# One queue for ScalarE's copies in the attention, and a reordered start, in a one-core encoder layer

## The chip, the core and the metric

The kernel runs on one core of a Trainium2 chip. A core has TensorE (PE, matrix products), VectorE (DVE), ScalarE (ACT), GpSimd (POOL) and SyncE (SP, which here only issues transfers), each with its own instruction stream, and 16 DMA engines. The metric is the device time of one execution in microseconds, lower is better.

## The reference

One layer of a streaming encoder on 2048 rows of width 1024, all in float32. In short:

```
mod = silu(c) @ w_ada + b_ada            # 6 x 1024: shift, scale, gate, twice
h = rmsnorm(x, g_norm1) * (1 + sc1) + sh1
q_sb, k_sb, v_sb, q_ca, k_ca, v_ca = split(h @ w_in)          # 8 heads of 64 each
o_sb = stick_breaking_attention(q_sb, k_sb, v_sb)             # strictly causal
o_ca = chunked_relpos_attention(rms(q_ca), rms(k_ca), v_ca, rel_bias)   # own chunk of 64 + 8 before it
x = x + gt1 * (concat(o_sb, o_ca) @ w_o)
h = rmsnorm(x, g_norm2) * (1 + sc2) + sh2
x = x + gt2 * (square(relu(h @ w1)) @ w2)
```

## The kernel before, in words

The rows are worked in four blocks of 512 (`TB`), in reversed order, transposed: 128 partitions hold 128 of the 1024 columns, so x of a block is eight tiles (`KT = 8`) of 128x512. Every float32 product of importance is made as three products of float32r parts: a copy to float32r ("hi", on ACT), the difference ("lo", on DVE or POOL, helper `split`), and `mm3`, which is hi by hi, hi by lo, lo by hi.

**Start.** TensorE first runs products of a tile of ones into a scrap bank (`keep_busy`, tile `idle`). Meanwhile SP loads the eight x tiles of block 3, with c between the sixth and the seventh, broadcast to 128 partitions (tile `cb`, 512 KB). ACT squares the x tiles, DVE adds the squares (`nsaa`), TensorE sums them over partitions (`norm_columns`, `pva`), DVE and POOL make the reciprocal root, ACT spreads it on a diagonal (`ndga`), and a product with ones gives it in all partitions (`norm_spread`, `pra`). ACT makes sigmoid(c), DVE multiplies by c into `cs`. The modulation columns are made as they are needed: `ada_column(j)` multiplies the 128x1024 tile `wa<j>` of the transposed w_ada by `cs` and sums along the row, one custom DVE instruction each (in the trace `wa<-wa,cs,bcol`). Then comes a loop over the eight k tiles: each needs its w_in columns (`wf`, split into `wfirst` and `wide`), two modulation columns (KT+k for the scale, k for the shift) and its normalized x (`ht`), and feeds 18 products into six banks (`pq`).

**Projections.** The other blocks and column groups follow, some postponed into the attention.

**Attention.** 112 units (stick-breaking `SB(h, g, c)`: head, query block, key block; chunked `CA(h, g)`) of four steps each, 448 steps, query blocks 2 and 3 first, then 1, then 0. At each step, in a written order: TensorE transposes the weights of the unit eight steps back (`wt`), the softmax work of this step runs (ACT `z`, DVE scan `p`, POOL `b` for SB; DVE, ACT `e`, POOL for CA), ACT and DVE split the transposed weights (`wth`, `wtl`), jobs left over from earlier steps run (list `soon`), TensorE multiplies weights with values (`acc`, two banks in turn) and makes the next scores, and `fill` puts as many products of postponed projections (`pf`, banks) and output projections (`po`, rows) as the plan's shares allow. A few jobs wait a counted number of steps in `later`.

When the last product of a head and query block is in, `finish` copies the two halves of its bank out, in two following steps (`otmp`, then `o`, ACT, 64x512 each), POOL adds them, and after every second head `keep` splits the pair (`os`) and stores it. Only after both copies can the bank be used again. Of a postponed projection's bank, ACT copies the hi part (`st` or `svf`) and a later job makes the lo part and stores it. A bank copy that meets a `finish` in one step waits a step; other meetings are let be. The output projections of blocks 2 and 3 also square their new rows and make the second norm's reciprocal root (`second`, `powers`, `spread`, `third`: tiles `pvm`, `nym`, `ndgm`, `prm`). The wrapper `Ordered` keeps an engine's instructions in the written order; SP's transfers in the attention go around it.

**After the attention.** The rest of block 1's output projection (`po`) runs as loads for block 0's output projection (`opm` from `scr_m`, weights `ow`) come in; then the MLP, by far the longest stage, with products of summed operands in the manner of Strassen.

Of the kernel before, what the change touches and what calls it, by code (L numbers as in the profile page):

```python
# [18 lines left out]
P = 128  # L19
# [60 lines left out]
def encoder_kernel(ctx, tc, xs, c, g1, g2, w_in, w_first, w_rest, gqk, bias, w_o, w1, w2, w_ada, b_ada, out):  # L80
# [163 lines left out]
    if True:  # L244
# [5 lines left out]
        padn.tile([P, 32], F32, tag="pad", name="padn")  # L250
# [5 lines left out]
        cb = stp.tile([P, D], F32, tag="bg", name="cb", bufs=2)  # L256
        cg = stp.tile([P, D], F32, tag="bg", name="cg", bufs=2)
# [247 lines left out]
        keep_busy(36, idle)  # L505
        act.activation(cg[:, 0:1], zero, AF.Sigmoid)
        for j in range(3):
            load_x_pair(3, j, osp)
        osp.dma_start(cb, c.partition_broadcast(P))
# [6 lines left out]
        def load_first(k):  # L516
            if k % 2 == 0:
                wraw.append(ring.tile([P, 2, 3, CW], F32, tag="r8", name=f"wf{k}"))
            if k:
                osp.dma_start(wraw[-1][:, k % 2], w_first[:, k])  # L520
            for j in (KT + k, k):
                adas[j] = adaw.tile([P, D], F32, tag="wa", name=f"wa{j}")
                osp.dma_start(adas[j], w_ada[j * P : (j + 1) * P, :])
            if not k:
                osp.dma_start(wraw[-1][:, k % 2], w_first[:, k])
# [16 lines left out]
        def silu(i):  # L542
            dve.tensor_tensor(*(t[:, i * TB : (i + 1) * TB] for t in (cs, cg, cb)), op=ALU.mult)
# [47 lines left out]
        first_w(1)  # L591
        for k in range(KT):
# [6 lines left out]
            for j in (KT + k + 1, k + 1) if k + 1 < KT else ():  # L599
# [7 lines left out]
            if k == 0:  # L607
                dve.tensor_copy(r3, p3)
# [12 lines left out]
            for m, p in enumerate(first):  # L621
                hi, lo = [w2s[k // 2][:, k % 2, l] if p == 2 else wide[:, k, l, p] for l in range(2)]
                for n in range(2):
                    cl = slice(n * P, (n + 1) * P)
                    mm3(
                        pss[2 * m + n], hi[:, cl], lo[:, cl], hts[3][k][:, 0, :], hts[3][k][:, 1, :],
                        k == 0, k == KT - 1,
                    )
# [80 lines left out]
    if True:  # L709
# [36 lines left out]
        def finish(u):  # L746
# [23 lines left out]
        def keep(u, o):  # L770
# [3 lines left out]
            q = act if u is units[-1] else sp  # L774
# [6 lines left out]
        class Unit:  # L781
# [26 lines left out]
            def values(self, j):  # L808
# [351 lines left out]
        def finish_row(g, n, ps, xr):  # L1160
# [93 lines left out]
        late, soon, first = [], [], []  # L1254
# [30 lines left out]
        def load(u):  # L1285
            need = (10,) if u.ca else (2, 3, 0, 1) + ((4,) if u.g == 0 else ())
            if u.g < 2:
                while not all((p, u.g) in have for p in need):
                    for job in soon:
                        job()  # L1290
                    soon.clear()
# [34 lines left out]
        for i in range(len(steps) + LAG):  # L1326
# [40 lines left out]
        while soon:  # L1367
            soon.pop(0)()
# [742 lines left out]
def _lay_out(i):  # L2111
# [6 lines left out]
        "c": i["c"][0],  # L2118
# [32 lines left out]
```

## Time and profile before

| | us |
|---|---|
| median of 3 runs (2524.98 to 2527.75) | 2527.54 |
| the profiled execution | 2525.42 |
| its span, first to last instruction | 2523.7 |
| PE busy, of the span | 2503.5 (99%) |
| DVE busy | 2034.2 (81%) |
| ACT busy | 1523.1 (60%) |
| POOL busy | 773.8 (31%) |

Times in the profile count from the span's start. A row of a timeline gives the start, the length, the engine, the operation with what it writes and reads, the form, how many, and in brackets the idle time of the engine before it with what ended it. A row of the waits names who waited for whom, the total, the number of times and the longest. A row of a table by stretches gives each engine's busy time and instruction count, then the granted TensorE clock, the busy share of the DMA engines and what they moved in GB/s. Most rows carry line 42, the wrapper's, so tiles tell instructions apart. A busy PE is not proof of useful work: at the start it is busy with the `idle` products.

### The profile page before, as it was taken

The numbers are of one execution on the slowest core, as the hardware profiler recorded it, in microseconds if no ns is written. First come the engines' busy times: TensorE is split into PE (matmuls) and PEld (weight loads), VectorE is DVE, ScalarE is ACT, GpSimd is POOL, SyncE is SP. The second block draws the span as 40 slices with busy tenths as digits, with TensorE's granted clock in tenths as the row PEclk, the third lists the DMA queues.
The fourth block names the chain that finished last, engine by engine and source line by source line (L and its number), as shares of the span: only waits on it lengthen the run. The fifth ranks groups of instructions, "written<-read, shape, count | busy, mean of one in ns | idle before, by whom it ended". The sixth has DMA issues, their size and how long they took to land.

```text
span 2523.7 us, 39531 instructions
## 1 busy us (share of the span) xinstructions
PE 2503.5 (99%) x12384; PEld 2093.8 (83%) x12384; DVE 2034.2 (81%) x3580; ACT 1523.1 (60%) x2917; POOL 773.8 (31%) x1156
## 2 busy tenths in 40 slices
PE   9999999999999999999999999999999999999999
PEld 7888888888888888888888888888888888888787
DVE  7656776887789888999858777779877859799998
ACT  6333424778876687666855555567555546576665
POOL 4330154776776677776620000000000000010000
PEclk9999999999999999999999999999999999999999
DMA  9879968789888788866787878996998996887882
GB/s 369 322 297 362 356 270 292 233 256 315 260 260 252 246 250 252 278 194 206 219 304 254 301 285 316 331 352 189 326 328 270 315 365 260 315 252 278 310 275 83
DMA packets 296547, 706.29 MB, mean 280 GB/s; under 512 B 32016, under 2 KB 88336, under 8 KB 284688
## 3 DMA queue, kind: packets, MB, share of 16 engines
q1 hardware_dynamic: 290432, 690.64, 79.5%
q0 software_dynamic: 4608, 8.39, 1.9%
q10 hardware_dynamic: 1296, 4.72, 0.5%
q8 instruction: 98, 1.61, 0.3%
q14 instruction: 113, 0.93, 0.1%
HBM read 476.61 MB, written 227.02 MB: 279 GB/s over the span
## 4 chain that ended last, share of the span: by engine, by line
PE 87%; DVE 7%; DMA 2%; ACT 1%; issue 1%; SPq 0%; POOL 0%; DVEq 0%; ACTq 0%; POOLq 0%
PE ps L42 25%; PE ps_s L42 15%; PE pt L42 11%; PE acc L42 7%; PE wt L42 7%; PE pf L42 5%; PE z L42 5%; PE po L42 4%; PE pq L42 3%; DVE opr L42 2%; PE pso L42 2%; PE cz L42 2%; DVE ol L42 1%; PE ct L42 1%; DVE r L42 1%
## 5 line engine op out<-in xcount | busy, mean ns | idle before, releaser
L42 ACT CAST wth<-wt 128x512 fp32r<-128x512 f32 (+3 forms) x544 | 257.7, 484 | 177.6 <-PE wt L42 164.7
L42 PE MATMUL ps<-h,opw 128*128 128x512 f32 x1512 | 358.6, 389 | 0.0
L42 DVE TENSOR_TENSOR wtl<-wt,wth 128x512 fp32r<-128x512 f32 (+3 forms) x544 | 291.7, 548 | 66.9 <-ACT wth L42 63.2
L42 POOL TENSOR_TENSOR b<-p 128x512 f32<-128x512 f32 (+1 forms) x320 | 292.0, 912 | 155.8 <-DVE p L42 103.5
L42 PEld LDWEIGHTS ps<-h,opw 128*128 128x128 f32 x1512 | 283.7, 188 | 58.8
L42 PE MATMUL pt<-w,ht 128*128 128x512 f32 x1248 | 288.2, 391 | 0.0
L42 PE MATMUL ps_s<-h,opw 128*128 128x512 f32 x1152 | 277.1, 389 | 0.0
L42 PEld LDWEIGHTS pt<-w,ht 128*128 128x128 f32 x1248 | 233.0, 188 | 47.7
L42 DVE TENSOR_TENSOR_SCAN p<-z,p,zero 128x512 f32<-128x512 f32 x192 | 245.5, 1280 | 20.1 <-ACT z L42 17.4
L42 PEld LDWEIGHTS ps_s<-h,opw 128*128 128x128 f32 x1152 | 216.0, 188 | 45.0 <-DVE cp L42 0.2
L42 ACT CAST opr<-r 128x512 fp32r<-128x512 f32 x280 | 174.3, 623 | 129.1 <-PE ps L42 71.4
L42 PE MATMUL ps<-opr,ol 128*128 128x512 f32 x960 | 222.0, 390 | 0.4 <-DVE opr L42 0.3
L42 PE MATMUL acc<-wth,v 128*128 128x512 f32 (+3 forms) x544 | 221.3, 410 | 0.2
L42 PEld LDWEIGHTS ps<-opr,ol 128*128 128x128 f32 x960 | 179.8, 188 | 40.2 <-DVE opr L42 1.9
L42 ACT ACTIVATE z<-z 128x512 f32<-128x512 f32 (+1 forms) x320 | 166.6, 521 | 54.1 <-PE z L42 49.5
L42 DVE TENSOR_TENSOR opr<-r,opr 128x512 fp32r<-128x512 f32 x280 | 188.5, 704 | 10.7 <-ACT opr L42 9.9
L42 PE MATMUL acc<-wtl,v 128*128 128x512 f32 (+3 forms) x544 | 185.5, 347 | 0.1
L42 PE MATMUL z<-k,q 128*128 128x512 f32 (+3 forms) x640 | 183.1, 368 | 1.5 <-DVE p L42 1.5
L42 POOL DMA_DIRECT2D scr_x<-txu x12 | 10.5, 879 | 546.6 <-ACT txu L42 529.2
L42 PE MATMUL ps<-oph,opv 128*128 128x512 f32 x768 | 175.5, 390 | 0.5 <-DVE txo L42 0.2
L42 PE MATMUL wt<-ident,b 128*128 128x128 f32 x1088 | 170.8, 272 | 1.5 <-DVE p L42 1.5
L42 PEld LDWEIGHTS wt<-ident,b 128*128 128x128 f32 x1088 | 137.2, 140 | 39.9 <-DVE p L42 2.2
(226 smaller groups left out, 5063.9 us busy)
## 6 DMA issues: line engine op xcount, KB each, us to landing
r<-scr_hid SPq DMA_DIRECT2D x80, 512.0 KB, 6.6
q<-scr_q SPq DMA_DIRECT2D x128, 256.0 KB, 5.2
w<-in_w_dram SPq DMA_DIRECT2D x64, 512.0 KB, 5.8
k<-scr_k SPq DMA_DIRECT2D x240, 128.0 KB, 4.3
v<-scr_v SPq DMA_DIRECT2D x120, 256.0 KB, 4.3
wa<-in_w_ada_dram SPq DMA_DIRECT2D x48, 512.0 KB, 6.3
ow<-scr_wo SPq DMA_DIRECT2D x24, 1024.0 KB, 6.5
l<-scr_t SPq DMA_DIRECT2D x20, 1024.0 KB, 7.4
```

What stands on the lines that cost most here:

```text
L42: return lambda *x, **y: self.tc.keep_in_program_order(f(*x, **y))
```

## The change

In the start, c is loaded as 128x8 columns (32 B to a partition) from ACT's queue instead of a broadcast of 512 KB on SP's; its silu is made on 8 columns, spread on eight diagonals by DVE and POOL, and eight products with ones give `cs`. There are 14 idle products in place of 36, and 9 more behind the new ones. The second tile's w_in part is loaded after its w_ada tiles, the first columns are made in another order, half the diagonal of the norm is made on POOL, the copy `r3` moves from DVE to ACT, and in the first two k tiles all products with the hi part of `ht` come before those with the lo part.

In the attention, `finish`, its second copy, `keep` and the bank copies go into one list, `heavy`, of which one runs per step, two when more than three wait, and none in the last two steps of a diagonal SB unit unless more than three wait. Block 0's chunked heads store through POOL's queue, except the last. The second norm of block 3 starts 14 steps after its last square instead of 3, and both norms' diagonals are made in two halves, a step apart, with the product one step later.

```diff
-        cb = stp.tile([P, D], F32, tag="bg", name="cb", bufs=2)
-        cg = stp.tile([P, D], F32, tag="bg", name="cg", bufs=2)
+        cg = stp.tile([P, KT, P], F32, tag="bg", name="cg", bufs=2)
...
-        keep_busy(36, idle)
-        act.activation(cg[:, 0:1], zero, AF.Sigmoid)
+        keep_busy(14, idle)
+        act.dma_start(ccol[:, 0], c)
+        act.activation(cg[:, 0, 0:1], zero, AF.Sigmoid)
         for j in range(3):
             load_x_pair(3, j, osp)
-        osp.dma_start(cb, c.partition_broadcast(P))
...
-            if k:
+            if k > 1:
                 osp.dma_start(wraw[-1][:, k % 2], w_first[:, k])
...
-            if not k:
+            if k < 2:
                 osp.dma_start(wraw[-1][:, k % 2], w_first[:, k])
...
+        act.activation(ccol[:, 1], ccol[:, 0], AF.Sigmoid)
+        dve.tensor_tensor(ccol[:, 1], ccol[:, 1], ccol[:, 0], op=ALU.mult)
+        for i, e in ((0, dve), (KT // 2, pool)):
+            ks = slice(i, i + KT // 2)
+            e.tensor_tensor(
+                cg[:, ks], ident.unsqueeze(1).to_broadcast([P, KT // 2, P]),
+                ccol[:, 1, ks].unsqueeze(2).to_broadcast([P, KT // 2, P]), op=ALU.mult,
+            )
+        for k in range(KT):
+            pe.matmul(cs[:, k * P : (k + 1) * P], ones, cg[:, k], start=True, stop=True)
+        keep_busy(9, idle)
...
-        more_squares(1, 6)
-        act.activation(cg, cb, AF.Sigmoid)
-        silu(0)
-        more_squares(6, KT)
-        silu(1)
+        more_squares(1, KT)
...
+        ada_column(KT, adas[KT])
         dve.tensor_scalar(v3, pv[:, 0:4], 1.0 / D, EPS, op0=ALU.mult, op1=ALU.add)
         pool.tensor_tensor(y3, v3, mhalf[:, :4], op=ALU.pow)
-        ada_column(KT, adas[KT])
+        ada_column(0, adas[0])
...
-        for i in range(4):
+        for i in range(2):
             act.activation(dg[:, i, :], ident, AF.Copy, scale=y3[:, i : i + 1])
-        ada_column(0, adas[0])
+            pool.tensor_tensor(dg[:, i + 2, :], ident, y3[:, i + 2 : i + 3].to_broadcast([P, P]), op=ALU.mult)
         first_scale(0)
+        ada_column(KT + 1, adas[KT + 1])
...
+        act.copy(r3, p3)
...
-            for j in (KT + k + 1, k + 1) if k + 1 < KT else ():
+            for j in ((KT + k + 1, k + 1) if k else (1,)) if k + 1 < KT else ():
...
-                dve.tensor_copy(r3, p3)
...
+                    if k > 1:
+                        mm3(ps, hi[:, cl], lo[:, cl], hts[3][k][:, 0, :], hts[3][k][:, 1, :], False, k == KT - 1)
+                        continue
+                    pe.matmul(ps, hi[:, cl], hts[3][k][:, 0, :], start=k == 0, stop=False)
+                    pe.matmul(ps, lo[:, cl], hts[3][k][:, 0, :], start=False, stop=False)
+            for m, p in enumerate(first) if k < 2 else ():
+                hi = w2s[k // 2][:, k % 2, 0] if p == 2 else wide[:, k, 0, p]
+                for n in range(2):
+                    pe.matmul(pss[2 * m + n], hi[:, n * P : (n + 1) * P], hts[3][k][:, 1, :], start=False, stop=False)
...
-                    wait({3: 6, 0: 2}.get(u.g, 4), lambda: keep(u, o))
-
-            soon.append(rest)
+                    wait({3: 6, 0: 2}.get(u.g, 4) - 1, lambda: heavy.append(lambda: keep(u, o)))
+
+            heavy.append(rest)
...
-            q = act if u is units[-1] else sp
+            q = act if u is units[-1] else pool if u.ca and u.g == 0 else sp
...
-                    done = lambda: finish(self)
-                    done.ends = True
-                    soon.append(done)
+                    soon.append(lambda: heavy.append(lambda: finish(self)))
...
-                    later.add(3, second)
+                    later.add(14 if g == 3 else 3, second)
...
-                dg = norm_diagonal(op, y, f"m{g}", op.tile([P, TB], F32, tag="otmp", name=f"ndgm{g}"))
-                later.add(2, lambda: third(dg))
+                dg = op.tile([P, TB], F32, tag="otmp", name=f"ndgm{g}").rearrange("p (a b) -> p a b", b=P)
+
+                def part(i):
+                    dve.tensor_tensor(
+                        dg[:, i : i + 2], ident.unsqueeze(1).to_broadcast([P, 2, P]),
+                        y[:, i : i + 2].unsqueeze(2).to_broadcast([P, 2, P]), op=ALU.mult,
+                    )
+
+                part(0)
+                later.add(1, lambda: part(2))
+                later.add(3, lambda: third(dg))
...
-            ends = any(hasattr(job, "ends") for job in done)
             for job in done:
-                if ends and hasattr(job, "bank"):
-                    soon.append(job)
+                if hasattr(job, "bank"):
+                    heavy.append(job)
                 else:
                     job()
+            short = front is not None and not front.ca and front.diag and fs > 1
+            for _ in range(max(0, len(heavy) - 3) if short else min(len(heavy), 1 + (len(heavy) > 3))):
+                heavy.pop(0)()
...
-        "c": i["c"][0],
+        "c": col(i["c"][0]),
```

More of the change, by code (lines that the diff above doesn't have):

```diff
@@ L249, in encoder_kernel @@
         padn = pa.enter_context(tc.tile_pool(name="padn", bufs=1))
-        padn.tile([P, 32], F32, tag="pad", name="padn")
+        ccol = padn.tile([P, 32], F32, tag="pad", name="padn")[:, : 2 * KT].rearrange("p (a k) -> p a k", k=KT)
         stp = pa.enter_context(tc.tile_pool(name="stp", bufs=6))
@@ L540, in more_squares @@
                 dve.tensor_tensor(acc, acc, sq, op=ALU.add)
-        def silu(i):
-            dve.tensor_tensor(*(t[:, i * TB : (i + 1) * TB] for t in (cs, cg, cb)), op=ALU.mult)
-        more_squares(1, 6)
-        act.activation(cg, cb, AF.Sigmoid)
-        silu(0)
-        more_squares(6, KT)
-        silu(1)
+        more_squares(1, KT)
         pv = norm_columns(pq, acc, "a3")
@@ L623, in encoder_kernel @@
                 for n in range(2):
[L624 to L628, printed above, removed]
+                    cl, ps = slice(n * P, (n + 1) * P), pss[2 * m + n]
+                    if k > 1:
[7 more added lines that the diff above has]
+                    pe.matmul(pss[2 * m + n], hi[:, n * P : (n + 1) * P], hts[3][k][:, 1, :], start=False, stop=False)
         free[0] += 4
@@ L1253, in encoder_kernel @@
         rest = 0
-        late, soon, first = [], [], []
+        late, soon, first, heavy = [], [], [], []
         def fill(part, more=0):
@@ L1288, in load @@
                 while not all((p, u.g) in have for p in need):
-                    for job in soon:
-                        job()
-                    soon.clear()
+                    while soon or heavy:
+                        (heavy or soon).pop(0)()
                     force(filler[0])
@@ L1366, in encoder_kernel @@
             value(u, j)
-        while soon:
-            soon.pop(0)()
+        while soon or heavy:
+            (heavy or soon).pop(0)()
         later.flush()
```

## The prediction

> **What bounds the kernel now.** I read the page first, then the stretches, then TensorE's waits, then the timeline where the change acts.
>
> ```profile
> span 2523.7 us, 39531 instructions
> PE 2503.5 (99%) x12384; PEld 2093.8 (83%) x12384; DVE 2034.2 (81%) x3580; ACT 1523.1 (60%) x2917; POOL 773.8 (31%) x1156
> ...
> L42 POOL DMA_DIRECT2D scr_x<-txu x12 | 10.5, 879 | 546.6 <-ACT txu L42 529.2
> ```
>
> TensorE is busy nearly throughout, so nothing that shortens another engine's work shortens the kernel by itself. The sum below was made against the execution with this span, which took 2525.42 us; the median of the runs is 2527.54, 2.1 us above it, and I carry the difference over to the median unchanged.
>
> ```profile
> 0.00:25.00 25.00, 20.75 (x131) 18.79 (x131) 16.13 (x28) 14.03 (x28) 8.12 (x17) 1.00 0.88 321
> 25.00:60.00 35.00, 35.00 (x155) 28.75 (x154) 28.49 (x45) 25.00 (x45) 20.45 (x17) 1.00 1.00 398
> 1200.00:1300.00 100.00, 97.29 (x589) 84.80 (x587) 66.82 (x224) 68.43 (x157) 55.22 (x44) 1.00 0.71 232
> ...
> PE po L42 <- DMA ow<-scr_wo: 2.3, 1, 2.3
> PE wt L42 <- DVE p L42: 2.2, 4, 1.1
> PE z L42 <- DVE p L42: 1.5, 5, 0.6
> PE po L42 <- DVE xr L42: 1.4, 1, 1.4
> ...
> PE prm L42 <- DVE xr L42: 0.5, 1, 0.5
> ```
>
> Real idle time lies at the start, and in a few holes of the attention: 7.9 us in the five rows of waits (first columns of the stretches: length, PE busy). After 25 us PE is full, so whatever brings the first useful product forward is kept, if the following data keep up. The start's 20.75 us of busy PE is mostly scrap products; there the place to read is the first `pq`.
>
> **The start, term by term.** The chain begins with c.
>
> ```profile
> 2.18 7.29 DMA cb<-in_c_dram
> ...
> 2.65 1.43 SPq L42 DMA_DIRECT2D xt<-in_xs_dram  x2
> 7.47 1.15 ACT L42 ACTIVATE nsqa<-xt 128x512 f32<-128x512 f32 x2 [0.23 <-DMA xt<-in_xs_dram]
> 9.56 1.06 ACT L42 ACTIVATE cg<-cb 128x1024 f32<-128x1024 f32 x1 [0.93 <-DMA cb<-in_c_dram]
> 10.52 1.13 ACT L42 ACTIVATE nsqa<-xt 128x512 f32<-128x512 f32 x2
> 11.26 1.48 DVE L42 TENSOR_TENSOR nsaa<-nsaa,nsqa 128x512 f32<-128x512 f32 x2
> 14.04 1.28 DVE L42 CUSTOM_DVE_ANT_0 wa<-wa,cs,bcol 128x1024 f32<-128x1024 f32 x1
> 15.87 1.28 ACT L42 ACTIVATE ndga<-ident,nya 128x128 f32<-128x128 f32 x4 [4.22 <-DVE nya L42]
> 17.82 0.75 DVE L42 SCALAR_TENSOR_TENSOR xt<-xt,aff,pra 128x512 f32<-128x512 f32 x1 [0.78 <-ACT wfirst L42]
> 19.37 0.50 PE L42 MATMUL pq<-ht,wfirst 128*128 128x512 f32 x1 [1.01 <-ACT ht L42]
> 20.37 1.40 PE L42 MATMUL pq<-ht,wfirst 128*128 128x512 f32 x5 [0.49 <-DVE ht L42]
> 26.56 2.88 PE L42 MATMUL pq<-ht,wide 128*128 128x512 f32 x12
> 29.28 1.52 PE L42 MATMUL pq<-ht,wfirst 128*128 128x512 f32 x6
> ...
> xt<-in_xs_dram SPq DMA_DIRECT2D x1, 256.0 KB, 7.5
> ```
>
> The broadcast lands at 2.18 + 7.29 = 9.47, the pair of x before it by 7.47: it takes 2.0 us of the transfers' time, and all behind it on SP's queue comes 2.0 earlier without it. The last x is issued at 3.43 and lands 7.5 later, at 10.9; in the new kernel at 8.9. Its square (1.13 / 2) and its sum (1.48 / 2) end at 10.2, where they now end at 12.74: -2.5. c itself, 128 rows of 32 B, is not in the trace; its landing lies between 0 and the 7.3 us that 512 KB took in a full queue, and 4 KB on an empty queue are nearest to the low end. Behind it come its silu (some 0.5), two half diagonals (up to 1.4, as `ndgm` on DVE further down) and 16 products of 128 columns (0.1 to 0.2 each, rows further down), some 5 us at most; it may land as late as 5.2 before `cs` is late for the first column at 10.2, so I count it as off the path. The old sigmoid (1.06) leaves ACT.
>
> From there to the diagonal's start at 15.87 it now takes 3.1 us, with one column (1.28) beside POOL's power. The new order on DVE puts another column ahead of the root, beside TensorE's sum over partitions; 0.3 of it may stick out. The diagonal starts at 10.2 + 3.1 + 0.3 = 13.6: -2.3. The diagonal is made by two engines, 0.64 in place of 1.28, if POOL's half is no slower; I take -0.5. The third column, moved ahead, costs DVE 1.28 us beside this diagonal and its spreading (17.82 - 15.87 = 1.95 now); it is hidden if its tile, moved ahead of the second w_in part on SP, has landed, and costs up to 1.3 if not. So the first scaling comes at 15.1 for 17.82, and the first product, 1.55 behind it as now, at 16.7 for 19.37: -2.7.
>
> Next the holes. From the first product to the third tile's (29.28) are 36 products; the pace is (29.28 - 26.56) / 12 = 0.227, so 8.2 us of work took 9.9. The products with the hi part first need not wait for DVE's lo part (the 0.49), and `r3` is copied by an idle ACT before the last two banks are wanted; what remains is ACT's chain to the second `ht`, some 0.4 by my addition. So the third tile starts at 16.7 + 8.2 + 0.4 = 25.3: -4.0. Bounds: -2.0 if the data set the pace (they moved by 2.0 only), -4.4 with no hole. The later columns' tiles land several us before they are needed by this reckoning, so I take **-3.9**.
>
> The number of scrap products must still bring TensorE to speed.
>
> ```profile
> 1.00:5.00 4.00, 3.81 (x18) 3.81 (x19) 1.00 0.77 227
> 7.00:11.00 4.00, 4.00 (x39) 4.00 (x38) 1.00 1.02 332
> ```
>
> In the first 4 us 18 scrap products ran (0.21 us each), later 39 (0.10): the array starts at half speed. 14 pairs plus the 8 new pairs plus 9 pairs keep it occupied to about 10.5, and the longest pause to the first useful product is some 1.5 us. [...] Were the array cold at 16.7, the products of the next few us would take 0.45 for 0.227: about +2.3 (the 4 us shown lost (39 - 18) x 0.11).
>
> **The attention, term by term.** Counting through the step plan in the code: 448 steps hold 64 `otmp`, 64 `o`, 32 `os` and 28 banks, and in 21 steps two of them meet. One such meeting, columns of the timeline as above:
>
> ```profile
> 502.44 0.58 ACT L42 COPY o<-acc 64x512 f32<-64x512 f32 x1
> 503.05 0.65 ACT L42 CAST svf<-pf 128x256 fp32r<-128x256 f32 x2
> ...
> 504.19 0.96 DVE L42 TENSOR_TENSOR_SCAN p<-z,masked 128x384 f32<-128x384 f32 x1 [1.04 <-ACT z L42]
> ...
> 1187.64 1.44 DVE L42 TENSOR_TENSOR ndgm<-ident,nym 128x512 f32<-128x512 f32 x1
> ...
> PE z L42 <- DVE p L42: 0.6, 1, 0.6
> PE wt L42 <- DVE p L42: 0.3, 1, 0.3
> ...
> L42 ACT COPY o<-acc 64x512 f32<-64x512 f32 x64 | 37.1, 579 | 1.3 <-POOL os L42 0.6
> ```
>
> Two copies ahead of `z` leave DVE idle 1.04 us, and TensorE then waits for DVE's `p`. All waits for `p` are 2.2 + 1.5 = 3.7 us; 1.1, the longest of `wt`, is the norm's (below), and of the 2.6 left, 0.9 lie at one meeting between 700 and 710 us alone (the two last rows of waits), the rest at smaller ones and at steps without any. After the change no step has two: between 0 and -2.6, I take **-1.2**.
>
> `ndgm` at 1187.64 holds DVE 1.44 us at the switch from SB to CA units, where `p` is just due: the 1.1. Its product's bank then makes the next row of `po` wait for `xr`: the 1.4. Eleven steps later (2 us each, from 448 steps in some 880 us) the switch is over, DVE is 67% busy by the stretch from 1200, and each half takes half. What is late next is again a bank, if a row ends within the two steps of that product: about 2 in 9 steps. Between +1.4 and -2.5, I take **-2.0**. For block 2 the product comes one step later and finds `xr` done, **-0.5** (the `prm` row).
>
> The end of the attention is the largest.
>
> ```profile
> 1267.61 0.80 SPq L740 DMA_DIRECT2D v<-scr_v  x2
> 1276.60 0.32 SPq L775 DMA_DIRECT2D scr_m<-os  x1
> 1277.02 2.17 SPq L42 DMA_DIRECT2D opm<-scr_m  x4
> 1279.29 0.39 SPq L42 DMA_DIRECT2D ow<-scr_wo  x1
> ...
> SPq L775 <- POOL os L42: 8.2, 1, 8.2
> ...
> 1270.00:1277.00 7.00, 6.79 (x49) 5.93 (x48) 4.34 (x12) 5.92 (x15) 2.64 (x3) 1.00 0.06 25
> ```
>
> SP waits 8.2 us with the store of a finished pair for POOL, and behind it stand four `opm` loads and the weights `ow`; the DMA engines lie at 0.06 busy meanwhile. Then four loads of 512 KB and `ow` with 1 MB come at once, and TensorE waits 2.3 for `ow`. With the store on POOL's queue, SP is free from 1268.4 (1267.61 + 0.80), the `opm` loads fall into the empty stretch, and `ow` no longer stands behind them: 2 MB at the 398 GB/s of the fullest stretch are 5.3 us, more than the 2.3 wanted. The three stores so moved cost POOL 0.88 each (the page's row), 2.6 in all, beside a POOL with 55 busy of 100 us; uncovered, the CA units' `e` comes later by that. Between 0 and -2.3, less up to 2.6: **-2.3** and **+0.3**.
>
> [...]
>
> The added wait: the queue can hold a copy back, and behind the two copies of a bank stand the products of the head after next. By the step plan the second copy comes at least one step ahead of that everywhere now; in the new order it falls into the same step at two places. Each costs between 0 and one copy, 0.58: **+0.6**, as PE has then nothing else in its order.
>
> Sum: -3.9 - 1.2 - 2.0 - 0.5 - 2.3 + 0.3 + 0.6 = **-9.0** us. That is 2516.4 for the profiled execution and 2518.5 for the median; since the waits' rows leave out the slower first product behind each pause, I say **2518**. A measurement of this kernel can tell about 0.2% (5.1 us) from no change.
>
> **Rivals.** (1) The attention nets nothing: TensorE's holes move to other steps, as half of the 2.6 of waits for `p` has no meeting behind it by my own term. Then only the start counts: 2527.5 - 3.5 = 2524, within 0.2%. (2) Slower, by one mechanism: copies held in the queue release the `acc` banks late. My count of two places rests on steps; ACT runs late within a step, so a margin of one step can turn into a wait. There are 63 such releases; at the copy's 0.58 each it is +36, and it decides from (9.0 + 5.1) / 63 = 0.22 us each. At 0.3 the time is 2518 + 19 = 2537. Against it: the row of `o` has ACT waiting 1.3 us in all, and PE's list of waits has none for `o` in its leading rows. (3) The wait for `ow` stays, because `ow` is held by its slot in the ring or by other loads: 2518 + 2.3 = 2520.3. [...] (4) The array is cold at the first product: 2518 + 2.3 = 2520.
>
> **How the numbers follow.** Chances: forecast 0.53, (1) 0.18, (2) 0.12, (3) 0.10, (4) 0.07. Faster holds the forecast, (3) and (4): 0.70; within 0.2% is (1): 0.18; slower is (2): 0.12. The range: at its low end all terms at their best, -4.4 - 2.6 - 2.5 - 0.5 - 2.3 = -12.3, and a little for a run at the lowest time shown: 2512. At its high end it takes in (1) with a start of only -2.0: 2526. It leaves out (2).
>
> **What would show it.** The first `pq` product near 16.7 and the third tile's near 25.3; no `p` waiting for `z` behind two copies; `ndgm` in two halves near 1210; the first `opm` before 1272 and no wait of `po` for `ow`. Wrong would be: `acc` waiting for ACT's `o` in many places, TensorE's products at double length after 16 us, or PE waiting for `wa` or `wf` between 20 and 60 us.

## The result and the profile after

The changed kernel takes 2519.44 us in the median (8 runs, 2518.34 to 2520.72), the kernel before 2525.55 us (8 runs, 2524.53 to 2527.75). The ratio is 0.9974, with a 95% interval of 0.9965 to 0.9983: faster by a quarter of a per cent, about 6.5 us. A second set of ten runs, taken beside the last experiments, gave 0.9973 (0.9964 to 0.9982). The profiled execution took 2519.46 us.

The page of the changed kernel, then TensorE's waits in the attention (in total, times, longest):

```profile
span 2517.8 us, 39521 instructions
PE 2501.8 (99%) x12374; PEld 2096.3 (83%) x12374; DVE 2034.4 (81%) x3581; ACT 1519.6 (60%) x2916; POOL 776.7 (31%) x1162
```
```profile
PE acc L42 <- ACT o L42: 3.0, 2, 1.9
PE z L42 <- DVE p L42: 2.1, 5, 0.8
PE wt L42 <- DVE p L42: 0.4, 1, 0.4
PE cz L42 <- DVE cols L42: 0.3, 1, 0.3
```

This list is complete for 411 to 1310 us. The waits for `ow` (2.3) and `xr` (1.4 and 0.5) are gone, those of `wt` for `p` fell from 2.2 to 0.4. New is `acc` waiting for `o`, and the waits of `z` for `p` have grown, at other places than before.

The start, from the timelines of TensorE, VectorE and ScalarE:

```profile
12.73 1.05 PE L42 MATMUL pva<-ones,nsaa 128*128 128x1 f32 x8 [1.40 <-DVE nsaa L42]
13.64 3.68 PE L42 MATMUL idle<-ones 128*128 128x128 f32 x18
20.10 0.73 PE L42 MATMUL pq<-ht,wfirst 128*128 128x512 f32 x2 [1.01 <-ACT ht L42]
...
5.76 0.69 DVE L42 TENSOR_TENSOR cg<-ident,padn 128x512 f32<-128x512 f32 x1
6.53 6.14 DVE L42 TENSOR_TENSOR nsaa<-nsaa,nsqa 128x512 f32<-128x512 f32 x7
...
5.25 0.21 ACT L42 ACTIVATE padn<-padn 128x8 f32<-128x8 f32 x1 [2.52 <-DMA padn<-in_c_dram]
7.70 2.19 ACT L42 ACTIVATE nsqa<-xt 128x512 f32<-128x512 f32 x4 [0.17 <-DMA xt<-in_xs_dram]
```

The squares are done at 7.70 + 2.19 = 9.89, but VectorE's seven additions run from 6.53 to 12.67. The first `pq` comes at 20.10, 0.7 later than before. From there to the third tile it is 8.3 us for 9.9 before, so that tile starts at 28.40 for 29.28 (first column of the table below).

The same kernel in stretches (length, busy time of TensorE, its loads, VectorE, ScalarE, GpSimd, then the granted clock):

```profile
10.80:14.22 3.42, 2.02 (x18) 1.82 (x17) 3.21 (x7) 0.00 (x0) 0.10 (x1) 1.00 1.03 414
14.22:17.63 3.41, 3.41 (x18) 3.41 (x18) 2.64 (x7) 1.79 (x5) 2.20 (x4) 0.50 1.04 411
614.96:618.38 3.42, 1.49 (x11) 1.27 (x10) 2.16 (x8) 2.40 (x6) 1.25 (x1) 1.00 0.99 216
618.38:621.79 3.41, 3.41 (x12) 2.82 (x11) 1.44 (x7) 0.88 (x3) 1.96 (x2) 0.50 1.05 338
```

Twice a stretch with a pause (1.40 and 1.93 us without a product) is followed by 3.41 us at half the clock. That is why the 18 scrap products behind `pva` took 3.68 us, for 2.25 before.

Where the time went, by landmarks on TensorE's timeline, for all kernels of this study (us). "Third tile" is the start of the first product of the third k tile, "first `z`" the start of the attention's scores, "first `pso`" that of block 0's output projection. The landmarks are those of one profiled execution each:

| kernel | third tile | to first `z` | first `z` to first `pso` | rest to the end | median of runs |
|---|---|---|---|---|---|
| before | 29.28 | 411.45 | 890.06 | 1222.2 | 2525.55 |
| changed | 28.40 | 410.75 | 885.83 | 1221.2 | 2519.44 |
| changed, second set | 27.58 | 409.92 | 884.20 | 1222.7 | 2519.21 |
| start alone | 28.59 | 411.00 | 891.58 | 1222.7 | 2526.34 |
| attention alone | 30.38 | 412.95 | 884.14 | 1222.1 | 2520.37 |
| heads first | 28.51 | 410.85 | 882.68 | 1221.2 | 2516.66 |
| closing copy later | 27.52 | 409.68 | 882.53 | 1225.1 | 2520.66 |
| heads first, closing copy later | 28.43 | 410.76 | 879.57 | 1224.6 | 2516.67 |
| store on SyncE | 29.02 | 411.18 | 887.07 | 1225.1 | 2523.05 |
| no pause at the start | 27.83 | 410.13 | 884.15 | 1221.8 | 2518.67 |
| squares summed on TensorE | 36.59 | 419.22 | 886.23 | 1221.6 | 2527.94 |
| three additions | 25.86 | 408.83 | 884.17 | 1221.2 | 2517.24 |
| heads first, no pause | 28.03 | 410.37 | 882.72 | 1221.5 | 2515.48 |
| heads first, last square on TensorE | 26.82 | 409.24 | 882.92 | 1221.0 | 2515.86 |

The kernel before had a median of 2525.85 to 2526.99 beside the experiments. TensorE is busy for 99% of the span, so a shift at one landmark is carried to the end unless a later stretch gives it back. One kernel can differ by 1.5 us in the last stretch from execution to execution, as the two rows of the changed kernel show (1221.2 and 1222.7).

### The profile page after: what moved, and what is told of

The parts are those of the page before. It is cut to its first block, busy times and chain, and to the rows that moved or that the text cites. A ratio compares the mean times of both kernels' runs of the same rounds, so it can differ in the third digit from the quotient of the medians.

```text
span 2517.8 us, 39521 instructions
## 1 busy us (share of the span) xinstructions
PE 2501.8 (99%) x12374; PEld 2096.3 (83%) x12374; DVE 2034.4 (81%) x3581; ACT 1519.6 (60%) x2916; POOL 776.7 (31%) x1162
## 4 chain that ended last, share of the span: by engine, by line
PE 94%; DVE 3%; ACT 1%; issue 1%; DMA 1%; POOL 0%; DVEq 0%; SPq 0%; ACTq 0%; POOLq 0%
PE ps L42 28%; PE ps_s L42 16%; PE pt L42 11%; PE acc L42 7%; PE wt L42 7%; PE pf L42 6%; PE po L42 5%; PE z L42 5%; PE pq L42 3%; PE pso L42 2%; PE cz L42 2%; PE ct L42 1%; PE px L42 1%; DVE p L42 1%; DVE opr L42 0%
## 5 line engine op out<-in xcount | busy, mean ns | idle before, releaser
L42 PEld LDWEIGHTS ps<-oph,opv 128*128 128x128 f32 x768 | 144.0, 188 | 31.0 <-DVE txo L42 0.6
```

Source lines behind the costliest of these rows:

```text
L42: return lambda *x, **y: self.tc.keep_in_program_order(f(*x, **y))
```

## The experiments

**Which half carries the gain.** One kernel has the changed start and the attention of before, the other the reverse. The edit is the diff shown earlier, cut at `finish`; its core, as the first of the two undoes it:

```diff
-                    wait({3: 6, 0: 2}.get(u.g, 4) - 1, lambda: heavy.append(lambda: keep(u, o)))
...
-            heavy.append(rest)
+                    wait({3: 6, 0: 2}.get(u.g, 4), lambda: keep(u, o))
...
+            soon.append(rest)
...
-            q = act if u is units[-1] else pool if u.ca and u.g == 0 else sp
+            q = act if u is units[-1] else sp
...
-                    later.add(14 if g == 3 else 3, second)
+                    later.add(3, second)
```

> The start of the changed kernel with the attention of the kernel before. Theory (the start nets almost nothing, because VectorE's chain of sums sets its end): the first `pq` near 20.1 us, the third tile's products near 28.4, and the whole about 0.7 to 0.9 us below the kernel before, which five rounds hardly tell from nothing. The prediction's account (start -3.9): about 4 us below. The holes at 615 and 959 us are absent, and `ow` keeps TensorE waiting 2.3 us.

> The start of the kernel before with the attention of the changed kernel. Theory: the attention carries the gain, -4.2 to -5.3 us against the kernel before. Rival (the attention nets nothing, the rest comes from elsewhere): within 1 us of it. The waits of TensorE's `acc` for ScalarE's `o` at two places (1.9 and 1.05 us) are there, and none for `ow`.

Measured against the kernel before: the start alone 0.9999 (0.9990 to 1.0008), the attention alone 0.9976 (0.9967 to 0.9985), that is 0 and about 6 us. The gain lies in the attention; the start is worth less than these runs can tell. The traces tell more. The start of before, in the attention-alone kernel, on TensorE's timeline:

```profile
13.30 1.05 PE L42 MATMUL pva<-ones,nsaa 128*128 128x1 f32 x8 [2.35 <-DVE nsaa L42]
14.22 3.88 PE L42 MATMUL idle<-ones 128*128 128x128 f32 x18
```

This is the same code as in the kernel before, yet its pause is 2.35 us and its third tile 1.1 us later (30.38), with half clock over those scrap products (0.53 granted from 14.3 to 17.6 us). So the old start can fall into the low clock too. At like clock the new start gains: 30.38 to 28.40 with the low clock in both (-2.0), 29.28 to 27.58 with full clock in both (-1.7). The start-alone kernel still has its `ow` wait (2.2 us), and its attention is 1.5 us longer than before (891.58). Its profiled execution had a mean granted clock of 0.998, for 1.0 before, and was at 0.58 from 14.3 to 17.6 us. One more stretch of 3.41 us at half clock would be enough for the 1.5; that is an estimate, and no row here shows where such a stretch lies.

**The copies of finished heads ahead of bank copies.** In the queue `heavy` a finished head's copy is put ahead of waiting bank copies:

```diff
-            heavy.append(rest)
+            urgent(rest)
+
+        def urgent(job):
+            heavy.insert(next((n for n, j in enumerate(heavy) if hasattr(j, "bank")), len(heavy)), job)
...
-                    soon.append(lambda: heavy.append(lambda: finish(self)))
+                    soon.append(lambda: urgent(lambda: finish(self)))
```

> The changed kernel with the copies of finished heads put ahead of waiting bank copies in the queue (still one to a step). Theory: TensorE's two waits of `acc` for `o`, 1.9 us at 615 and 1.05 us at 959, go, and with the first of them the stretch of half clock that follows it (3.41 us at 0.5, worth about 1.5 us): 3 to 4.5 us below the changed kernel. Rival (the bank copies that are now late make the CA units' rows late and stall there): within 1 us of the changed kernel, with new waits for `txu` or `z`. If the pause did not cause the low clock, 0.5 shows again near 618 us.

Ratio to the kernel before 0.9964 (0.9951 to 0.9976), 2516.66 us: 2.5 to 3 us below the changed kernel. The two intervals overlap, but each of the five runs (2516.47 to 2518.27) is below each of the first eight of the changed kernel (from 2518.34). ScalarE's timeline near 615 us shows the two copies change places; first the changed kernel, with TensorE's wait, then the experiment:

```profile
614.65 0.57 ACT L42 CAST stf<-pf 128x512 fp32r<-128x512 f32 x1
616.80 0.58 ACT L42 COPY o<-acc 64x512 f32<-64x512 f32 x1
...
617.44 0.50 PE L42 MATMUL acc<-wth,v 128*128 128x512 f32 x1 [1.93 <-ACT o L42]
```
```profile
615.40 0.58 ACT L42 COPY o<-acc 64x512 f32<-64x512 f32 x1
617.47 0.58 ACT L42 CAST stf<-pf 128x512 fp32r<-128x512 f32 x1
```
```profile
600.00:700.00 100.00, 99.85 (x620) 87.84 (x619) 74.57 (x272) 84.67 (x214) 73.39 (x72) 1.00 0.90 278
```

The bank copy had taken the one place of its step, and `o` came a whole step (2.15 us) later. With the order turned, the wait at 615 and the half clock behind it are gone (1.00 granted from 600 to 700 us, for 0.98 in the changed kernel). The wait near 958 stayed, at 1.0 us, as there no bank copy stands in the way. ScalarE's timeline there, before, then in the changed kernel with TensorE's wait:

```profile
954.39 0.58 ACT L42 COPY otmp<-acc 64x512 f32<-64x512 f32 x1
954.87 0.26 ACT L42 ACTIVATE z<-z 128x128 f32<-128x128 f32 x1
956.47 0.58 ACT L42 COPY o<-acc 64x512 f32<-64x512 f32 x1
```
```profile
953.87 0.26 ACT L42 ACTIVATE z<-z 128x128 f32<-128x128 f32 x1 [0.29 <-PE z L42]
957.77 0.58 ACT L42 COPY otmp<-acc 64x512 f32<-64x512 f32 x1
959.67 0.58 ACT L42 COPY o<-acc 64x512 f32<-64x512 f32 x1
...
960.30 0.49 PE L42 MATMUL acc<-wth,v 128*128 128x512 f32 x1 [1.05 <-ACT o L42]
```

The `z` of 128x128 is the last step of a diagonal SB unit. Before, the two copies ran in the unit's last two steps, `otmp` ahead of that `z` and `o` behind it. The changed kernel runs none of the list in these two steps, so both copies come two steps later. No run lifts this rule alone. The expectation was right on the first place and wrong on the second.

**The closing copy a step later.** The change had moved `keep`'s copy one step forward; here it gets the full count again:

```diff
-                    wait({3: 6, 0: 2}.get(u.g, 4) - 1, lambda: heavy.append(lambda: keep(u, o)))
+                    wait({3: 6, 0: 2}.get(u.g, 4), lambda: heavy.append(lambda: keep(u, o)))
```

> The changed kernel with the copy that closes a unit's head put into the queue one step later, the full count of steps after the unit, as it was before the change. Theory: ScalarE no longer waits 1.7 us for GpSimd's sum at that copy, and TensorE's waits of `z` for `p` at 1101, 1104 and 1161 us (0.7, 0.3 and 1.0) go: about 2 us below the changed kernel. Rival (these holes come from the meeting of norm and pass, not from the copy): same time, holes unmoved.

> The changed kernel with both edits of the queue: finished heads' copies ahead of bank copies, and the closing copy a step later. Theory (the two remove different holes): 0 to 2 us below the one with finished heads' copies first alone, all of TensorE's waits for `o` and for `p` after 1000 us gone. Rival (the later closing copy pushes the next finished head's copy behind it): a wait of `acc` for `o` of about 1 us at a step without one before, and no gain over that kernel.

In the changed kernel ScalarE waits for GpSimd's sum ahead of this copy, and `z` behind it is late (ScalarE, then TensorE):

```profile
1099.69 0.62 ACT L42 CAST os<-o 128x512 fp32r<-128x512 f32 x1 [1.67 <-POOL o L42]
...
1102.23 0.62 PE L42 MATMUL z<-k,q 128*128 128x384 f32 x2 [0.54 <-DVE p L42]
```

The stretch around it, in the changed kernel and with the copy later:

```profile
1095.00:1170.00 75.00, 73.50 (x409) 60.64 (x408) 68.49 (x85) 48.56 (x92) 54.41 (x90) 1.00 0.61 199
```
```profile
1095.00:1170.00 75.00, 75.00 (x420) 62.69 (x419) 71.18 (x89) 49.86 (x94) 56.19 (x92) 1.00 0.66 214
```

The holes are gone, as expected, and the attention is 1.7 us shorter than in the second set of the changed kernel. But the kernel isn't faster: 2520.66 us, 0.9980 (0.9971 to 0.9989). With heads first the attention is shorter still, 879.57 us, and the time is that of heads first alone, 2516.67 for 2516.66. In both the gain is given back behind the attention, in the last column but one of the table (1225.1 and 1224.6 for 1221.2). TensorE's longest wait there, for the kernel with both edits:

```profile
PE pso L42 <- DMA opm<-scr_m: 1.5, 2, 1.2
```

The `opm` loads of the next stage did not come earlier by as much, and a TensorE that is there 3 us earlier than with heads first alone waits for them. With a wait of 0.7 for ScalarE at `ps_s` the list names 2.2 of the 3.4 us; the rest isn't in it. The closing-copy kernel alone lost 3.9 against one execution of the changed kernel and 2.4 against the other; where was not settled (its list has 0.3 for `opm` and 1.0 for ScalarE at `ps_s`, which theirs don't have). The rival of the second expectation, a new wait of `acc` for `o` at another step, did turn up in the closing-copy kernel: three such waits, 3.8 us in all.

**The stores back on SyncE's queue.**

```diff
-            q = act if u is units[-1] else pool if u.ca and u.g == 0 else sp
+            q = act if u is units[-1] else sp
```

> The changed kernel with the three stores of block 0's finished pairs back on SyncE's queue. Theory (SyncE waits with the store, and the loads behind it start late): the first `opm` load is issued near 1277 us again, TensorE waits some 2.3 us for `ow`, and the kernel is 2 to 2.5 us slower than the changed one. [...]

SyncE's timeline in the changed kernel, then SyncE's and TensorE's in the experiment:

```profile
1266.80 1.85 SPq L42 DMA_DIRECT2D opm<-scr_m  x4
```
```profile
1266.31 0.80 SPq L750 DMA_DIRECT2D v<-scr_v  x2
1273.56 0.32 SPq L785 DMA_DIRECT2D scr_m<-os  x1
1273.98 2.16 SPq L42 DMA_DIRECT2D opm<-scr_m  x4
...
1287.25 11.16 PE L42 MATMUL po<-fx,ow 128*128 128x512 f32 x48 [1.04 <-DMA ow<-scr_wo]
```

The store again holds SyncE for 6.5 us with the loads behind it. TensorE's wait for `ow` is back, at 1.0 and not 2.3, and the attention is 1.24 us longer (887.07 for 885.83; behind 618 us both are slowed alike, four products of `wt` taking 1.05 and 1.06 us there, for 0.60 with heads first). In the runs the kernel is about 3 us slower (0.9986, 0.9977 to 0.9995, for 0.9974 and 0.9973; the intervals overlap a little). The part beyond 1.24 lies behind the attention, in 1225.1 for 1221.2 or 1222.7; the profile doesn't show that the store causes that part. As far as the 1.24 go, the issue of the store (0.32 us) is less than the loss: the store waits on SyncE's queue, and the `opm` loads behind it are issued at 1273.98 for 1266.80.

**No pause ahead of the sums over partitions.**

```diff
             pe.matmul(cs[:, k * P : (k + 1) * P], ones, cg[:, k], start=True, stop=True)
-        keep_busy(9, idle)
+        keep_busy(16, idle)
```

> The changed kernel with 16 pairs of scrap products behind the spread of c in place of 9, so that TensorE has no pause of 1.4 us or more ahead of the sums over partitions. Theory (the pause takes the clock to half for 3.41 us, which makes the 18 scrap products behind `pva` take 3.0 to 3.9 us in place of 2.25): clock 1.0 throughout 12 to 20 us, first `pq` at 19.0 to 19.3, about 0.9 below the changed kernel, third tile near 27.4. Rival (the low clock has another cause, or VectorE sets the diagonal all the same): low clock still there, or first `pq` at 20.1.

TensorE's timeline:

```profile
13.07 1.05 PE L42 MATMUL pva<-ones,nsaa 128*128 128x1 f32 x8 [0.53 <-DVE nsaa L42]
13.98 2.25 PE L42 MATMUL idle<-ones 128*128 128x128 f32 x18
19.50 1.21 PE L42 MATMUL pq<-ht,wfirst 128*128 128x512 f32 x4 [1.01 <-ACT ht L42]
```

The scrap products are back at 2.25 us and the first `pq` is 0.6 earlier though VectorE's sums ended 0.3 later here. The time is 2518.67 us, ratio 0.9967 (0.9955 to 0.9980): below the changed kernel as expected, but by less than these runs can tell.

**What VectorE's additions cost.** First the sums were moved to TensorE altogether, a product over partitions for each square:

```diff
-                dve.tensor_tensor(acc, acc, sq, op=ALU.add)
...
+            for i in range(4):
+                pe.matmul(
+                    pv[:, i : i + 1], sq[:, i * P : (i + 1) * P], ones[:, 0:1],
+                    start=k == 0 and i == 0, stop=k == KT - 1, skip_group_check=True,
+                )
```

> The changed kernel with the sums of squares over the k tiles taken by TensorE (each square accumulated into the same bank by its products over partitions), VectorE's seven additions left out. Theory (those additions, one after another, hold the start: the last x lands at 8.9 but the last addition ends at 12.7): `pva` complete near 10.4, the diagonal 2 to 3 us earlier, the first `pq` at 16 to 17 for 20.1, third tile near 25; 2 to 4 us below the changed kernel. Rival (the landing of the column weights or the columns on VectorE hold it just as long): first `pq` earlier, but third tile still at 27.5 to 28.4, and the time within 1 us.

It did not come: 2527.94 us, 1.0004 (0.9995 to 1.0012), the first `pq` at 28.29. TensorE's timeline and two stretches:

```profile
12.40 0.95 PE L42 MATMUL pva<-ones,nsqa 128*128 128x1 f32 x8
```
```profile
12.60:16.00 3.40, 3.40 (x32) 3.40 (x32) 0.84 (x2) 0.00 (x0) 0.00 (x0) 1.00 1.03 414
16.00:19.40 3.40, 3.40 (x18) 3.40 (x18) 0.00 (x0) 0.00 (x0) 0.00 (x0) 0.50 0.46 186
```

The eight products of one square, of one column each, keep TensorE for 0.81 us until the next product can start (0.95 to their modelled end), no less than the addition (0.79) that they replace, and the scrap products between two squares take another 0.53. The clock fell to half for 10.2 us, from 16.00, though TensorE had no pause at all (3.40 of 3.40 us busy in the stretch ahead). So this kernel tested TensorE's small products and not VectorE's sums. The next one tests the sums; it leaves four of the seven additions out, so its norm is that of half the columns:

```diff
-                dve.tensor_tensor(acc, acc, sq, op=ALU.add)
+                if k < 4:
+                    dve.tensor_tensor(acc, acc, sq, op=ALU.add)
```

> The changed kernel with four of VectorE's seven additions of squares at the start left out (the k tiles 4 to 7 are missing from the first norm, so its values are others); ScalarE still makes all squares. Theory (VectorE's additions set the end of the start): the last addition ends near 9.2 in place of 12.7, `pva` begins at 11.3 behind the scrap products, no pause and no low clock, first `pq` near 17.8, third tile near 26.1, 2 to 2.5 us below the changed kernel. Rival (the column weights' landing or the columns hold the products as long): first `pq` earlier, third tile at 27.5 or later.

The timelines of VectorE, ScalarE and TensorE:

```profile
6.74 2.96 DVE L42 TENSOR_TENSOR nsaa<-nsaa,nsqa 128x512 f32<-128x512 f32 x3
...
19.60 1.28 DVE L42 CUSTOM_DVE_ANT_0 wa<-wa,cs,bcol 128x1024 f32<-128x1024 f32 x1 [0.55 <-DMA wa<-in_w_ada_dram]
21.41 1.60 DVE L42 TENSOR_TENSOR ht<-xt,ht 128x512 fp32r<-128x512 f32 x1 [0.53 <-ACT ht L42]
...
17.49 0.41 ACT L42 CAST wfirst<-wf 128x256 fp32r<-128x256 f32 x1 [0.41 <-DMA wf<-in_w_first_dram]
...
17.12 1.20 PE L42 MATMUL pq<-ht,wfirst 128*128 128x512 f32 x4 [1.01 <-ACT ht L42]
25.86 0.51 PE L42 MATMUL pq<-ht,wfirst 128*128 128x512 f32 x1
26.73 1.43 PE L42 MATMUL pq<-ht,wfirst 128*128 128x512 f32 x5 [0.37 <-DVE ht L42]
```

The sums end at 9.7, the first `pq` comes 2.16 us earlier than in the second set of the changed kernel (19.28, full clock too), and the third tile's first product 1.72 (25.86 for 27.58; the theory had 26.1, the rival 27.5 or later). Its second product comes only 1.08 earlier, at 26.73, as it waits for VectorE's lo part of `ht`. Two things in the rows made that part late. ScalarE waited 0.41 for w_in columns (`wf`), which put VectorE's subtraction for the second tile half a microsecond back, and this subtraction took 1.60 us, for 0.69 in the changed kernel (at 23.86). VectorE's wait of 0.55 for the column weights `wa` fell into time in which it would have waited for ScalarE. So the additions held the first products, and half of what their absence brings is given back behind them. The time is 2.0 us below the changed kernel on the same chip, with 0.9965 (0.9951 to 0.9978).

**Putting it together.** The kernel as changed was run again beside these, then with the two edits heads first and no pause together, and with heads first and the last square alone taken by TensorE (with 4 and 4 pairs of scrap products around it in place of 9). The core of the last one:

```diff
+                if k < KT - 1:
+                    dve.tensor_tensor(acc, acc, sq, op=ALU.add)
+            return sq
...
+            part = (sq7, acc)[i // 4][:, i % 4 * P : (i % 4 + 1) * P]
+            pe.matmul(pv[:, i % 4 : i % 4 + 1], part, ones[:, 0:1], start=i == 0, stop=i > 3, skip_group_check=True)
```

> The changed kernel itself, unedited, as the base for the three beside it on the same chip. All theories: 0.25% below the kernel before, 2519 to 2521 us. By the reading of the clock in the runs so far (a stretch of 3.41 us in which TensorE does nothing for about half is followed by one at half clock), its pause of 1.4 to 2.1 us ahead of `pva` and its pause of 1.9 us near 615 may or may not be followed by a low clock, by where they fall; a low clock after each of them whatever the place would speak for a simple length.

> The changed kernel with two edits together: finished heads' copies ahead of bank copies in the queue, and 16 pairs of scrap products in place of 9 behind the spread of c. Theory (the two act at different places and add up): 3.5 to 4.5 us below the changed kernel, clock 1.0 from 5 us to the end. Rival (what the first brings is given back where the loads for the next stage land, as the kernel with the closing copy a step later showed): no more than 2.5 below.

> The kernel with finished heads' copies first, and at the start VectorE adds six squares while TensorE takes the last one straight into the same sums over partitions, with scrap products of 4 and 4 pairs around it. Theory: VectorE's last addition ends 0.8 earlier (near 11.9), no pause of over 1 us, no low clock before 20 us; first `pq` at 18.3 to 18.8, third tile near 27, and 1 us below the kernel with finished heads' copies first alone. Rival (products of one column count as idle for the clock): low clock within 12 to 18 us, first `pq` at 19.2 or later.

The changed kernel again: 2519.21 us (ten runs, 2516.82 to 2521.74). In this execution neither pause was followed by a low clock, though the pauses were 2.10 and 1.9 us:

```profile
12.86 1.05 PE L42 MATMUL pva<-ones,nsaa 128*128 128x1 f32 x8 [2.10 <-DVE nsaa L42]
13.77 2.25 PE L42 MATMUL idle<-ones 128*128 128x128 f32 x18
19.28 1.20 PE L42 MATMUL pq<-ht,wfirst 128*128 128x512 f32 x4 [1.01 <-ACT ht L42]
```
```profile
612.71:616.12 3.41, 1.98 (x16) 1.74 (x14) 3.35 (x10) 3.38 (x9) 1.14 (x1) 1.00 0.98 278
616.12:619.53 3.41, 2.91 (x16) 2.56 (x17) 1.61 (x7) 1.09 (x3) 0.71 (x2) 1.00 1.04 254
```

Heads first and no pause: 2515.48 us (2515.25 to 2516.27), 0.9959 (0.9947 to 0.9972), 3.7 us below the changed kernel, and each of its five runs below each of the ten. The two edits add up, as expected. It has the lowest median here, 0.41% below the kernel before. Its clock was full up to the drain in the profiled execution (1.00 in all stretches to 2510 us), as expected. The last square on TensorE brings what was expected at the start: first `pq` at 18.53, third tile at 26.82 (0.76 earlier, one addition's 0.79), no low clock (the 18 scrap products behind `pva` took 2.25 us, and the mean clock was 1.0). Its time, 2515.86 us (2514.86 to 2516.19), can't be told from the other's.

## Why the prediction was right and wrong

The prediction was 2518 with 2512 to 2526, the direction right, the size less so: it summed to -9.0 us, and the runs of before and after differ by 6.1 in their medians and about 6.5 by the ratio. That the median came within 1.4 us is in part luck: the three runs of before had a median (2527.54) 2.0 above that of eight. The sum for the attention came near by luck too: two terms that failed, 4.7 us worse together, met holes that closed further than forecast or that it had not named.

| term | predicted | measured | from |
|---|---|---|---|
| start, third tile | -3.9 | -1.7 (full clock), -2.0 (half clock in both) | four traces above |
| attention, first `z` to first `pso` | -5.1 | -5.9 (full clock), -4.2 (half clock at 618) | table |
| two copies in one step | -1.2 | -2.6 | holes at `p`, 420 to 730 us |
| norm of block 3 and block 2 | -2.0, -0.5 | -2.4, -0.3 | holes at `po`, `cz`, `prm` |
| end of the attention (`ow`) | -2.3 | -2.4 (gone); undone: 1.24 | traces; store on SyncE |
| late `acc` release | +0.6 | +3.3, and the half clock behind it some 1.6 | heads first |
| closing copy a step earlier | not counted | +2.0 | closing copy later |

The holes are measured from start to start of TensorE's products, each less the median of the same two kinds, holes of over 0.15 us alone, in the traces of before and of the changed kernel's second set. Over the whole attention all excess of over 0.04 us falls from 22.7 to 16.7 us, the -5.9 again; the waits' list falls from 8.3 to 5.8 only, since it leaves out the short ones and the slower products behind a pause (four of `pq` took 1.04 us from start to start behind the 1.01 us at 20.10 in the changed kernel, and 0.91 without a pause at 24.32). The rows below the second add up to -2.4 without the half clock. Those on two copies in one step and on the norm are read from the traces alone; no run takes them back one by one. Beside them, holes at 959, 1248 and 1276 us that the prediction hadn't named give another 1.5, the rest lies in short ones. The 1.6 is 885.83 less 884.20, two executions of one kernel.

**The start** failed in the step by which the last square and the last sum "end at 10.2", as if they followed the last x at once. They can't: VectorE makes seven additions one behind the other at 0.79, it begins them at 6.53, and the first took 1.37 beside GpSimd's half of the diagonal of c (1.54 us from 5.81), for 0.69 of the others. They end at 12.67. c landed at 5.2, 4.4 us after its issue, the very limit up to which the prediction counted it as off the path. Of the 2.3 us between the forecast third tile (25.3) and the one at full clock (27.58), the kernel with three additions takes back 1.7 at that tile's first product. Behind it a second step fails, "The later columns' tiles land several us before they are needed": with the sums early, `wa` and `wf` are both waited for, and by the second product 1.1 of the 2.16 us gained at the first `pq` are lost again. Right were the holes behind the first product: 36 products took 8.3 us, where the prediction had 8.2 + 0.4.

**The scrap products** were judged enough, with a pause of "some 1.5 us" held harmless. The pause was 1.40 us and was followed by half clock for 3.41 us. The rival of a cold array named its price at 2.3 us for the first useful products; what came was milder, some 0.8 us (20.10 for 19.28), as the low stretch ended at 17.63, ahead of the first `pq`.

**The late release** was the mis-sized term. There were two places, as forecast (615 and 958 us), but each was priced at one copy, 0.58. The copy `o` stands at the end of ScalarE's work of its step, so TensorE waits for that work as well: 1.9 and 1.05 us, and the first one was followed by half clock (0.50 from 618.38). The first copy was a step late by a bank copy, the second two steps late by the rule of no copies at the end of a diagonal unit. The rival of late releases at all 63 places didn't come: the list has two.

**The closing copy** has no term in the prediction. It went into the queue one step earlier, ahead of GpSimd's sum, and the wait of ScalarE (1.67 us) is in front of `z`. That is what the prediction itself saw on SyncE's queue (8.2 us of waiting for GpSimd, with the loads behind it waiting too), not applied to this line.

**The end of the attention** and the bursts came as said: `opm` issued at 1266.80 (forecast before 1272), no wait for `ow`, and `ndgm` in two halves at 1212 and 1215 with the old stalls gone. But taking the store back costs 1.24 us there and not the 2.3 of the wait, and the +0.3 for GpSimd's issuing was not taken apart by a run.

## What to carry to other kernels

When a change spreads copies over steps, price a copy that falls into the step of the product that needs it at all the work its engine does ahead of it in that step, and not at its own length, and let the copies that free an accumulator go ahead of those that only fill a buffer. When an early landing is to bring a stage forward, count the serial chain of the engine behind it instruction by instruction, and look for the transfer that becomes late next. And leave no pause on TensorE that scrap products could fill: pauses of 1.4 and 1.9 us cost some 0.8 and 1.6 us more here by the half clock behind them. A gain ahead of a stage whose loads do not come earlier with it can be given back there.

## What the hardware showed beyond this

Whether half clock followed a pause went, in these executions, with where the pause fell. The profiled execution of the changed kernel has three low stretches, from 14.22, from 618.38 and, in the drain, from 2516.19 us, and all three begin on one grid of 3.413 us, the length of the first two: from the end of the first (17.63) to the begin of the second it is 600.75 us, 176 such periods, and from there to the third 1897.81, 556 of them. Away from the start, the pause of 1.9 us at the same product was followed by half clock in that execution, where it lay whole in one period (1.93 us idle), and not in the second set, where the two stretches of 3.41 us shown above hold 1.43 and 0.50 us of it. Two more stretches of this length with much idle time, 1.51 us from 1286.35 in the kernel before and 1.62 us from 611.83 in the kernel with three additions, were followed by full clock. At the start, 1.16 us idle beside 1.05 us of products of one column was followed by half clock (heads first, from 11.76), and the kernel with all squares on TensorE fell to half clock with no idle time at all. In these two runs products of one column didn't keep the clock full; with the last square on TensorE, where two groups of them took 1.05 us each, it stayed full. What sets the clock is not in the trace.

The granted clock on record is not all: from 1 to 5 us of the kernel before the view gives 1.00, though the 18 scrap products there took 0.21 us each, for 0.10 from 7 to 11 us. The first clock record of that trace begins at 6.35 us.

The low stretches go with longer times. Of the 18 executions of the changed kernel, three had a mean granted clock of 1.0 and took 2517.9 us on average, the 15 at 0.998 or 0.999 took 2519.6. All five of the kernel with heads first and no pause were at 1.0. Of the 62 executions of the kernel before beside the experiments, 28 were at 1.0 (2525.7), 23 at 0.999 (2526.7) and 11 at 0.998 (2527.5).

The small load of c, 128 rows of 32 B, took 4.4 us from its issue (0.79) to its use (5.2), while SyncE issued five loads of x beside it (0.79 to 3.21).
